# The opening of a streaming encoder step: the first two feature tiles as groups of their own, half-size loads and another order of the first steps

## The chip, the cores and the metric

The kernel runs on one core of a Trainium2 chip. The metric is the time of one execution on the device, in microseconds. A core has five engines that run their own instruction queues: TensorE (PE in the profile; its weight loads are PEld), VectorE (DVE), ScalarE (ACT), GpSimd (POOL) and SyncE (SP), which here issues the large loads. Engines wait for each other through semaphores; within an engine, instructions run in the order in which they were written.

## The reference

One layer of a hybrid encoder for two request groups, 256 frames of a new stream and 32 frames of a running one, all in fp32 with a width of 2048. What matters here is its beginning:

```python
def mixer_layer(x, c, conv_hist, ret_state, pos, ada_w, ada_b, g_pre, ...):
    mod = jax.nn.silu(c) @ ada_w + ada_b
    shift, scale, gate = jnp.split(mod, 3, axis=-1)
    h = rms_norm(x, g_pre) * (1.0 + scale[:, None]) + shift[:, None]
    proj = h @ w_in
    gb, gc, gu, zc, q, k, v, zr, ma, mb = jnp.split(proj, SPLIT_POINTS, axis=-1)
    ...
```

Behind it come a gated short convolution, a retention over eight heads, two branch products, an output product and a gated residual. The change touches none of these.

## The kernel before

**Tiles.** All 288 frames are kept with the features on the partitions: 16 feature tiles `kt` of 128 x 288. Products are made in fp32r, a rounded fp32, and each fp32 operand is split into a high and a low part, so that every product of a weight block and a tile of h is three matmuls: high by high (line 374), high by low (375) and low by high (378). Weights are split on the chip: ScalarE casts a piece of 128 x 1024 to `whi` (line 282), VectorE subtracts to get `wlo` (line 289). h is split in the same way into `hh` (line 346) and `hl` (line 352).

**The first stage.** Before the large loops the kernel makes h, and as each pair of feature tiles of h comes into being, multiplies it with the columns of q, k and of half of v (`FIRST`, three pieces of 1024 columns), and adds the results in SBUF in `firsts`. Eight groups `g` of two feature tiles (`GS = 2`) run one after the other. For each group the kernel needs 4 MB of `ada_w` (`ada_first`, four loads of 1 MB, each with four of the 16 feature tiles of c and the columns of shift and scale of this group) and 3 MB of `w_in` (`w_first`, three loads `u` of 1 MB, each two pieces). `modulate` (line 306) multiplies silu(c) with a load of `ada_first`, 8 instructions a load, and the last one copies the row to SBUF (`modrow`, line 310). `gather_mod` (line 316) turns it to the partitions, `factors` (lines 328 to 330) make a multiplier and an addend, `new_h` (lines 342 to 346) makes h and hh, `low_parts` hl.

**A block.** `multiply(i)` takes one load of `w_first`, that is, block (g, u). It goes in four steps j of two output tiles (a `pair` of PSUM banks, three of which turn). A step has 12 products; of each output tile they are: four with `whi` (both feature tiles with hh and hl), then `wlo` of the first feature tile, then `wlo` of the second. VectorE adds the pair into `firsts` (line 383; in group 0 it is copied, line 381). Then the step cuts further pieces ahead, as many as a small table says: `usual` is one after j = 1 and one after j = 3, and `rare` lists the blocks that differ. The blocks of a group run as (g, 0), (g, 1), the modulation of group g + 1, then (g, 2), in which h of the next group is made ahead of step 1; (g + 1, 0) follows at once.

**Order.** In this stage the order of all instructions on TensorE, ScalarE, VectorE and SyncE is the order of the Python program. Nine buffers `raw` hold the loads (the three tiles of x first), five each hold `whi` and `wlo`; load i + 8 is issued at the head of iteration i.

**The opening.** x is loaded in three pieces: `x[2]` (the 32 sample rows), `x[0]`, `x[1]`. ScalarE sums their squares (`square`, line 407), `norm` makes the mean (line 202, VectorE), the power -1/2 (line 204, GpSimd) and scales x (line 412, VectorE); `turn_x` transposes a piece on TensorE (line 422) and copies it to `xT` (line 424, VectorE or ScalarE). Lines 401 and 403 transpose the small vectors.

Of the kernel before, what the change touches and what calls it, by code (L numbers as in the profile page):

```python
# [36 lines left out]

GS, MOD = 2, 4
NG = NK // GS

# [52 lines left out]
def packed(c_prompt, c_sample, ada_b, state_conv, conv_w, conv_b, norm_pre, ada_w, w_in):  # L93


    rows = lambda *a: np.concatenate([np.reshape(v, (-1, P)) for v in a])
    small = rows(c_prompt, c_sample, ada_b[0, D:2 * D])
    table = rows(state_conv, conv_w, conv_b, norm_pre, ada_b[0, :D])
    a = ada_w[0, :, :2 * D].reshape(NK // MOD, MOD, P, 2, NG, GS * P)
    a = a.transpose(4, 0, 2, 1, 3, 5).reshape(NG, NK // MOD, P, MOD * 2 * GS * P)  # L100
    w = np.stack([w_in[0, :, c:c + PIECE] for c in FIRST]).reshape(len(FIRST), NG, GS, P, PIECE)
    w = w.transpose(1, 0, 3, 2, 4).reshape(NG, len(FIRST), P, GS * PIECE)
    return [np.ascontiguousarray(v) for v in (small, table, a, w)]


@with_exitstack
def hybrid_step(ctx: ExitStack, tc, x_prompt, x_sample, c_prompt, c_sample, state_conv, state_ret,
# [115 lines left out]
    with ExitStack() as phase:  # L223
# [25 lines left out]
        NU = len(FIRST)  # L249
        loads = [(True, 0, s) for s in range(NK // MOD)]  # L250
        for g in range(NG):
            m = [(True, g + 1, s) for s in range(NK // MOD)] if g + 1 < NG else []
            w = [(False, g, u) for u in range(NU)]
            loads += w[:2] + m + w[2:]
        raws, parts_of, mod_ps, state_of = {}, {}, {}, {}

        def load(i):
            if i >= len(loads):
                return
            is_mod, g, u = loads[i]  # L260
            raw = buffer("raw", KH * WC, F32, RAW, MORE_RAW)
            src = (ada_first if is_mod else w_first)[g, u]

            n = 2 if g == 0 and (is_mod or u == 0) else 1
            m = KH * WC // n
            for j in range(n):
                nc.sync.dma_start(out=raw[:, j * m:(j + 1) * m], in_=src[:, j * m:(j + 1) * m])
            if is_mod:
                raws[i] = raw.rearrange("p (k s c) -> p k s c", k=MOD, s=2)
            else:  # L270
                raws[i] = raw.rearrange("p (k c) -> p k c", k=GS)

        to_cut = [(i, k) for i, (is_mod, _, _) in enumerate(loads) if not is_mod for k in range(GS)]

# [9 lines left out]

        def cut_low():
            if half_cut:
                i, k, hi = half_cut.pop(0)
                lo = buffer("wlo", PIECE, F32R, PARTS, MORE_PARTS)
                V.tensor_tensor(out=lo, in0=raws[i][:, k], in1=hi.bitcast(F32), op=ALU.subtract)  # L289
                parts_of[i, k] = hi, lo  # L290

        def cut():
# [3 lines left out]
        def modulate(i):  # L296

            _, g, u = loads[i]
            if u == 0:
                mod_ps[g] = small_tile()  # L300
            pm, v = mod_ps[g], raws.pop(i)
            for k in range(MOD):
                kt = u * MOD + k
                for s in range(2):
                    at = 32 * (2 * (kt % 2) + s)
                    nc.tensor.matmul(pm[at:at + 32, :GS * P], cs[:, kt, :], v[:, k, s, :], start=kt < 2, stop=kt >= NK - 2,  # L306
                                     tile_position=(0, at))
            if u == NK // MOD - 1:
                ms = st.tile([P, GS * P], F32, name="modrow", tag="modrow", bufs=2)
                A.copy(out=ms, in_=pm[:, :GS * P])  # L310
                mod_ps[g] = ms

        def gather_mod(g):
            ms, po = mod_ps.pop(g), small_tile()
            for f in range(GS):
                nc.tensor.matmul(po[:, 4 * f:4 * f + 4], ms[:, f * P:(f + 1) * P], pick, start=True, stop=True)
            state_of[g] = po

        def factors(g):
            ks = slice(g * GS, (g + 1) * GS)  # L320
            mod = state_of[g][:, :4 * GS].rearrange("p (f s b) -> p f s b", s=2, b=2)
            mul = st.tile([P, GS, 2], F32, name="mul", tag="mul", bufs=2)
            add = st.tile([P, GS, 2], F32, name="add", tag="add", bufs=2)

            def each(v):
                return v.unsqueeze(2).broadcast_to([P, GS, 2])

# [5 lines left out]
        def new_h(g):  # L333
            mul, add = state_of[g]
            state_of[g] = hs = []
            for f in range(GS):
                h = st.tile([P, T], F32, name="h", tag="h", bufs=GS)
                kt = g * GS + f
                on_v = g == 0 and f == 1
                for b, c in enumerate((slice(0, TP), slice(TP, T))):  # L340
                    if on_v or (g == 0 and b):
# [4 lines left out]
                (V.tensor_copy if on_v else A.copy)(out=hh[:, kt, :], in_=h)  # L346
                hs.append(h)

        def low_parts(g):
            for f, h in enumerate(state_of.pop(g)):  # L350
                kt = g * GS + f
                V.tensor_tensor(out=hl[:, kt, :], in0=h, in1=hh[:, kt, :].bitcast(F32), op=ALU.subtract)  # L352


        usual, rare = {1: 1, 3: 1}, {(0, 0): {1: 1, 2: 1}, (0, 1): {3: 2}, (0, 2): {1: 1, 2: 1}, (1, 0): {1: 1, 2: 1, 3: 1}}

        def multiply(i):

            _, g, u = loads[i]
            parts = [parts_of.pop((i, k)) for k in range(GS)]  # L360
            cuts = rare.get((g, u), usual)
            nxt = u == NU - 1 and g + 1 < NG
            for j in range(NF // 2):
                if nxt and j == 1:
                    cut_high()
                    gather_mod(g + 1)
# [3 lines left out]
                for f in range(2):  # L370
                    ps, fs = pp[:, f, :T], slice((2 * j + f) * P, (2 * j + f + 1) * P)
                    for k, (hi, lo) in enumerate(parts):
                        kt = g * GS + k
                        nc.tensor.matmul(ps, hi[:, fs], hh[:, kt, :], start=k == 0, stop=False)  # L374
                        nc.tensor.matmul(ps, hi[:, fs], hl[:, kt, :], start=False, stop=False)  # L375
                    for k, (hi, lo) in enumerate(parts):
                        kt = g * GS + k
                        nc.tensor.matmul(ps, lo[:, fs], hh[:, kt, :], start=False, stop=k == GS - 1)  # L378
                sums = firsts[:, u * NF + 2 * j:u * NF + 2 * j + 2, :]
# [19 lines left out]
        xT = st.tile([P, NK, T], F32, name="xT")  # L399
        vp = small_tile()  # L400
        nc.tensor.transpose(out=vp[:, :3 * NK], in_=crows, identity=ident[:3 * NK, :3 * NK])
        vp2 = small_tile()
        nc.tensor.transpose(out=vp2[:, :NR * NK], in_=vrows, identity=ident)

# [8 lines left out]

        def turn_x(t):

            n = rows_of[t]
            m = 1024 // n if n < P else 8
            m = min(m, NK)
            for k0 in range(0, NK, m):
                pp = pair_tile().rearrange("p a b -> p (a b)")  # L420
                for k in range(m):
                    nc.tensor.transpose(out=pp[:, k * n:(k + 1) * n], in_=x[t][:n, (k0 + k) * P:(k0 + k + 1) * P],  # L422
                                        identity=ident[:n, :n])
                (V.tensor_copy if k0 or t == 2 else A.copy)(out=xT[:, k0:k0 + m, t * P:t * P + n],
                                                  in_=pp[:, :m * n].rearrange("p (k n) -> p k n", k=m))

        square(2)
        cv = vp[:, :2 * NK].rearrange("p (b k) -> p k b", b=2)
# [7 lines left out]
        ab1 = st.tile([P, NK], F32, name="ab1")  # L436
        V.tensor_scalar(out=ab1, in0=vp[:, 2 * NK:3 * NK], scalar1=1.0, scalar2=None, op0=ALU.add)
        V.tensor_copy(vecs, vp2[:, :NR * NK].rearrange("p (r k) -> p r k", r=NR))
        norm(0)
# [12 lines left out]
        new_h(0)  # L452
        cut_high()
        low_parts(0)
        cut_low()
        cut_low()

# [404 lines left out]
```

## Time and profile before

| | us |
|---|---|
| median of 3 runs (1353.58 to 1354.37) | 1353.85 |
| the profiled execution | 1354.2 |
| its span, from the first to the last instruction | 1352.4 |

The mean granted clock of TensorE over the span is 0.994. On the page, the busy time of an engine is also given as a share of the span, and the span is cut into 40 slices of 33.8 us, in which a digit is the busy share in tenths. The chain that ended last, by engine and by line:

```profile
PE 96%; DVE 2%; ACT 1%; DMA 1%; issue 0%; DVEq 0%; POOL 0%; POOLq 0%; ACTq 0%
PE acc L162 26%; PE acc L161 26%; PE acc L164 26%; PE pair L374 4%; PE pair L378 4%; PE pair L375 4%; PE small L306 2%; PE aux L665 1%; PE aux L508 0%; PE aux L509 0%; PE aux L510 0%; DVE wlo L289 0%; PE pair L422 0%; PE aux L610 0%; DMA state<-in_state_ret_dram 0%; PE aux L804 0%
```

The `acc` lines are the large loops behind the first stage, the `pair` lines the first stage. In the other views a row of a timeline gives the start, the time taken, the engine, the line, the operation, output <- inputs, shapes and a count; in brackets is the idle time of the engine ahead of it and what ended it. A row of windows gives for a stretch the busy time of PE, PEld, DVE, ACT and POOL, with the number of instructions, then the granted clock of TensorE, the busy share of the DMA engines and GB/s.

### The profile page before, as it was taken

What the parts mean: (1) busy time and instruction counts of PE and PEld (TensorE: products, weight loads), DVE (VectorE), ACT (ScalarE), POOL (GpSimd) and SP (SyncE); (2) the same over time, 40 slices, a digit from 0 to 9 for tenths busy, and PEclk for the clock granted to TensorE, in tenths of its full rate; (3) what the DMA queues carried; (4) which work ended last, traced back from release to release, by engine and by line L of the source; (5) the groups of instructions that cost most, each with busy time, mean ns of one, the idle gap of its engine ahead of it and who ended that gap; (6) DMA issues with size and microseconds to landing.
All of it is one profiled execution on the core that took longest, in us unless ns stands there. A gap on an engine that the chain in (4) does not pass through costs nothing.

```text
span 1352.4 us, 24163 instructions
## 1 busy us (share of the span) xinstructions
PE 1324.2 (98%) x10266; PEld 1302.0 (96%) x10266; DVE 834.1 (62%) x1380; ACT 547.5 (40%) x812; POOL 10.0 (1%) x18
## 2 busy tenths in 40 slices
PE   6999999999999999999999999999999999999996
PEld 5899899999999999999999999999999999999995
DVE  4667679865557766756877875555555544655443
ACT  4443346654444333333333333333333334334441
POOL 0000000000000000000000000000000000000000
PEclk8999999999999999999999999999999999999998
DMA  9988765455455675675666665544546355557431
GB/s 381 376 320 332 298 226 163 129 164 166 144 172 172 211 249 187 200 236 188 199 208 217 203 207 183 180 163 157 183 160 188 126 173 170 157 169 244 156 94 70
DMA packets 209116, 267.80 MB, mean 198 GB/s; under 512 B 5072, under 2 KB 199936, under 8 KB 201872
## 3 DMA queue, kind: packets, MB, share of 16 engines
q1 hardware_dynamic: 202784, 256.13, 55.9%
q10 hardware_dynamic: 6224, 10.13, 2.5%
q8 instruction: 80, 1.31, 0.4%
q14 instruction: 28, 0.23, 0.1%
HBM read 261.75 MB, written 4.49 MB: 197 GB/s over the span
## 4 chain that ended last, share of the span: by engine, by line
PE 96%; DVE 2%; ACT 1%; DMA 1%; issue 0%; DVEq 0%; POOL 0%; POOLq 0%; ACTq 0%
PE acc L162 26%; PE acc L161 26%; PE acc L164 26%; PE pair L374 4%; PE pair L378 4%; PE pair L375 4%; PE small L306 2%; PE aux L665 1%; PE aux L508 0%; PE aux L509 0%; PE aux L510 0%; DVE wlo L289 0%; PE pair L422 0%; PE aux L610 0%; DMA state<-in_state_ret_dram 0%; PE aux L804 0%
## 5 line engine op out<-in xcount | busy, mean ns | idle before, releaser
L127 DVE TENSOR_TENSOR wlo<-raw,whi 128x1024 fp32r<-128x1024 f32 x336 | 410.4, 1222 | 364.6 <-ACT whi L126 364.3
L126 ACT CAST whi<-raw 128x1024 fp32r<-128x1024 f32 x336 | 352.6, 1050 | 518.6 <-PE acc L162 471.3
L161 PE MATMUL acc<-hh,whi 128*128 128x288 f32 x1920 | 524.4, 296 | 0.9 <-DVE firsts L383 0.9
L162 PE MATMUL acc<-hl,whi 128*128 128x288 f32 x1920 | 525.0, 295 | 0.0
L161 PEld LDWEIGHTS acc<-hh,whi 128*128 128x128 f32 x1920 | 360.8, 188 | 1.4 <-ACT whi L126 1.1
L162 PEld LDWEIGHTS acc<-hl,whi 128*128 128x128 f32 x1920 | 361.1, 188 | 0.1
L164 PE MATMUL acc<-hh,wlo 128*128 128x288 f32 x1920 | 329.4, 293 | 0.0
L164 PEld LDWEIGHTS acc<-hh,wlo 128*128 128x128 f32 x1920 | 281.1, 188 | 0.0
L374 PE MATMUL pair<-hh,whi 128*128 128x288 f32 x384 | 110.3, 302 | 2.3 <-ACT hh L346 1.7
L375 PE MATMUL pair<-hl,whi 128*128 128x288 f32 x384 | 109.1, 299 | 0.1
L649 DVE SCALAR_TENSOR_TENSOR gbc<-raw,sc,gbc 128x256 f32<-128x256 f32 x240 | 100.5, 476 | 4.0 <-DMA raw<-in_ada_w_dram 3.9
L383 DVE TENSOR_TENSOR firsts<-pair,firsts 128x576 f32<-128x576 f32 x84 | 62.3, 753 | 39.4 <-PE pair L378 39.3
L378 PE MATMUL pair<-hh,wlo 128*128 128x288 f32 x384 | 84.1, 299 | 1.9 <-DVE wlo L289 1.8
L374 PEld LDWEIGHTS pair<-hh,whi 128*128 128x128 f32 x384 | 73.3, 191 | 5.8 <-issue 2.9
L375 PEld LDWEIGHTS pair<-hl,whi 128*128 128x128 f32 x384 | 73.4, 191 | 0.3 <-DVE hl L352 0.3
L162 PE MATMUL acc<-ml,whi 128*128 128x288 f32 x256 | 70.6, 297 | 0.0
L161 PE MATMUL acc<-mh,whi 128*128 128x288 f32 x256 | 70.1, 296 | 0.0
L161 PE MATMUL acc<-ch,whi 128*128 128x288 f32 x256 | 70.0, 296 | 0.0
L162 PE MATMUL acc<-yl,whi 128*128 128x288 f32 x256 | 70.0, 295 | 0.0
L161 PE MATMUL acc<-yh,whi 128*128 128x288 f32 x256 | 69.9, 296 | 0.0
L162 PE MATMUL acc<-cl,whi 128*128 128x288 f32 x256 | 69.5, 294 | 0.0
L378 PEld LDWEIGHTS pair<-hh,wlo 128*128 128x128 f32 x384 | 63.0, 191 | 3.1 <-DVE wlo L289 3.1
(182 smaller groups left out, 1316.3 us busy)
## 6 DMA issues: line engine op xcount, KB each, us to landing
raw<-in_w_in_dram SPq DMA_DIRECT2D x120, 1024.0 KB
raw<-in_w_branch_dram SPq DMA_DIRECT2D x32, 1024.0 KB
raw<-in_ada_first_dram SPq DMA_DIRECT2D x28, 1024.0 KB
raw<-in_w_first_dram SPq DMA_DIRECT2D x23, 1024.0 KB
raw<-in_ada_w_dram SPq DMA_DIRECT2D x16, 1024.0 KB
raw<-in_w_out_dram SPq DMA_DIRECT2D x16, 1024.0 KB
raw<-in_ada_first_dram SPq DMA_DIRECT2D x8, 512.0 KB
raw<-in_x_prompt_dram SPq DMA_DIRECT2D x2, 1024.0 KB
```

Of the source, the lines that this page charges most:

```text
L126: A.copy(out=hi, in_=src)
L127: V.tensor_tensor(out=lo, in0=src, in1=hi.bitcast(F32), op=ALU.subtract)
L161: nc.tensor.matmul(ps, hi[:, k, fs], xh[:, k0 + k, :], start=first and k == 0, stop=False)
L162: nc.tensor.matmul(ps, hi[:, k, fs], xl[:, k0 + k, :], start=False, stop=False)
L164: nc.tensor.matmul(ps, lo[:, k, fs], xh[:, k0 + k, :], start=False, stop=last and k == n - 1)
L306: nc.tensor.matmul(pm[at:at + 32, :GS * P], cs[:, kt, :], v[:, k, s, :], start=kt < 2, stop=kt >= NK - 2, tile_position=(0, at))
L374: nc.tensor.matmul(ps, hi[:, fs], hh[:, kt, :], start=k == 0, stop=False)
L375: nc.tensor.matmul(ps, hi[:, fs], hl[:, kt, :], start=False, stop=False)
L378: nc.tensor.matmul(ps, lo[:, fs], hh[:, kt, :], start=False, stop=k == GS - 1)
L383: V.tensor_tensor(out=sums, in0=pp[:, :, :T], in1=sums, op=ALU.add)
L649: V.scalar_tensor_tensor(out=ga[:, b], in0=raw[:, k], scalar=sc[:, kt, b:b + 1], in1=ga[:, b], op0=ALU.mult, op1=ALU.add)
L665: nc.tensor.matmul(pg[:, b, :], ones32, ga[:, b, :], start=True, stop=True)
```

## The change

The groups become `[[0], [1], [2, 3], [4, 5], ..., [14, 15]]`: tiles 0 and 1 are groups of their own, so there are nine groups, and what was group g of two tiles is now group g + 1. A one-tile group needs two loads of `ada_first` of 1 MB (eight feature tiles of c each, 128 columns of shift and of scale) and three loads of `w_first` of half a MB (one piece each); half-size loads take a whole buffer. A modulation step of such a group is half as wide and there are as many of them (32) as for two tiles. The arrays are packed on the host accordingly.

```diff
-GS, MOD = 2, 4
-NG = NK // GS
+GS = 2
+GROUPS = [[0], [1]] + [[k, k + 1] for k in range(2, NK, GS)]
+NG = len(GROUPS)
...
+        def shares(g):
+            return [(True, g, s) for s in range(2 * len(GROUPS[g]))] if g < NG else []
+
+        loads = shares(0)
         for g in range(NG):
-            m = [(True, g + 1, s) for s in range(NK // MOD)] if g + 1 < NG else []
+            m = shares(g + 1)
             w = [(False, g, u) for u in range(NU)]
             loads += w[:2] + m + w[2:]
...
-            n = 2 if g == 0 and (is_mod or u == 0) else 1
-            m = KH * WC // n
+            m = 2 if g == 0 and is_mod else 1
+            m = size // m
...
-        usual, rare = {1: 1, 3: 1}, {(0, 0): {1: 1, 2: 1}, (0, 1): {3: 2}, (0, 2): {1: 1, 2: 1}, (1, 0): {1: 1, 2: 1, 3: 1}}
+        usual = {1: 1, 3: 1}
+        rare = {(0, 0): {}, (0, 1): {0: 1, 2: 1, 3: 1}, (0, 2): {}, (1, 0): {}, (1, 1): {3: 3}, (1, 2): {}}
...
+                ahead = nxt and j == 1 and cuts.get(1)
                 if nxt and j == 1:
-                    cut_high()
+                    if ahead:
+                        cut_high()
                     gather_mod(g + 1)
...
                 if nxt and j == 1:
                     low_parts(g + 1)
-                    cut_low()
-                for _ in range(cuts.get(j, 0) - (nxt and j == 1)):
+                    if ahead:
+                        cut_low()
+                for _ in range(cuts.get(j, 0) - (1 if ahead else 0)):
                     cut()
...
+        def busy(ps, n):
+            for _ in range(n):
+                nc.tensor.transpose(out=ps, in_=ident, identity=ident)
...
+        busy(vp2[:, P:2 * P], 8)
         square(2)
...
-        V.tensor_copy(vecs, vp2[:, :NR * NK].rearrange("p (r k) -> p r k", r=NR))
+        turn_x(2, 1)
+        nc.tensor.transpose(out=vp2[:, :NR * NK], in_=vrows, identity=ident)
         norm(0)
-        turn_x(2)
+        V.tensor_copy(vecs, vp2[:, :NR * NK].rearrange("p (r k) -> p r k", r=NR))
+        turn_x(0, 2)
         norm(1)
-        turn_x(0)
         modulate(0)
-        turn_x(1)
+        turn_x(1, 2)
         for i in range(NBUF - len(x), NBUF - 1):
             load(i)
-        for i in range(1, NK // MOD):
-            modulate(i)
+        modulate(1)
+        idle = pair_tile()
+        busy(idle[:, 0, :P], 4)
         cut_high()
         gather_mod(0)
         factors(0)
+        busy(idle[:, 1, :P], 10)
         new_h(0)
-        cut_high()
+        low = low_steps(2)
+        next(low)
         low_parts(0)
-        cut_low()
-        cut_low()
+        next(low)
+        cut()
```

`low_steps(2)` subtracts the first `wlo` in two halves. In group 0 the sample columns of h are made on VectorE and all else of h and hh on ScalarE; before, VectorE also made the second tile. `busy` writes spare transposes of the identity, 22 in all, that nothing reads.

The opening on VectorE, from the constant ab1 to the copies of xT; `ms` and `raw` are the mean and the scaling of a piece of x, `vecs` the turned vectors. Before:

```order
L437 TENSOR_SCALAR ab1_146<-small_130 128x16
L438 COPY vecs_76<-small_132 128x128
L202 TENSOR_SCALAR ms_149<-ss_127 128x1
L412 TENSOR_SCALAR raw_102<-raw_102,rstd_151 128x2048
L424 COPY xT_129<-pair_154 128x16x32
L202 TENSOR_SCALAR ms_172<-ss_127 128x1
L412 TENSOR_SCALAR raw_103<-raw_103,rstd_174 128x2048
L424 COPY xT_129<-pair_187 128x8x128
L424 COPY xT_129<-pair_216 128x8x128
```

The same place in the changed kernel:

```order
L465 TENSOR_SCALAR ab1_150<-small_127 128x16
L451 COPY xT_126<-pair_152 128x16x32
L207 TENSOR_SCALAR ms_171<-ss_124 128x1
L440 TENSOR_SCALAR raw_102<-raw_102,rstd_173 128x2048
L469 COPY vecs_76<-small_128 128x128
L451 COPY xT_126<-pair_187 128x8x128
L207 TENSOR_SCALAR ms_197<-ss_124 128x1
L440 TENSOR_SCALAR raw_103<-raw_103,rstd_199 128x2048
L451 COPY xT_126<-pair_229 128x8x128
```

The copy of the transposed sample rows now stands ahead of the mean and the scaling of x[0], and the second copy of x[0] ahead of the mean and the scaling of x[1].

The seam from block (1, 0) to (1, 1) before, tiles 2 and 3, on VectorE; pair_601 is the last pair of (1, 0), pair_621 the first of (1, 1):

```order
L383 TENSOR_TENSOR firsts_85<-pair_583,firsts_85 128x576
L289 TENSOR_TENSOR wlo_599<-raw_290,whi_597 128x1024
L383 TENSOR_TENSOR firsts_85<-pair_601,firsts_85 128x576
L289 TENSOR_TENSOR wlo_617<-raw_453,whi_615 128x1024
L383 TENSOR_TENSOR firsts_85<-pair_621,firsts_85 128x576
```

The products of the first output tile of (1, 1) on TensorE before:

```order
L374 MATMUL pair_621<-hh_77,whi_579 128x288
L375 MATMUL pair_621<-hl_78,whi_579 128x288
L374 MATMUL pair_621<-hh_77,whi_597 128x288
L375 MATMUL pair_621<-hl_78,whi_597 128x288
L378 MATMUL pair_621<-hh_77,wlo_581 128x288
L378 MATMUL pair_621<-hh_77,wlo_599 128x288
```

The block reads wlo_581 and wlo_599; the split behind the sum of pair_601, the last of (1, 0), is wlo_617 of another load.

The same seam in the changed kernel, (2, 0) to (2, 1), also tiles 2 and 3, on VectorE; pair_689 is the last pair of (2, 0):

```order
L307 TENSOR_TENSOR wlo_673<-raw_466,whi_671 128x1024
L407 TENSOR_TENSOR firsts_85<-pair_675,firsts_85 128x576
L407 TENSOR_TENSOR firsts_85<-pair_689,firsts_85 128x576
L307 TENSOR_TENSOR wlo_705<-raw_466,whi_703 128x1024
L407 TENSOR_TENSOR firsts_85<-pair_709,firsts_85 128x576
```

And on TensorE, the products of the first output tile of (2, 1):

```order
L399 MATMUL pair_709<-hh_77,whi_671 128x288
L400 MATMUL pair_709<-hl_78,whi_671 128x288
L399 MATMUL pair_709<-hh_77,whi_703 128x288
L400 MATMUL pair_709<-hl_78,whi_703 128x288
L402 MATMUL pair_709<-hh_77,wlo_673 128x288
L402 MATMUL pair_709<-hh_77,wlo_705 128x288
```

The split that stands behind the sum of pair_689 is now one that this block reads.

More of the change, by code (lines that the diff above doesn't have):

```diff
@@ L98, in packed @@
     table = rows(state_conv, conv_w, conv_b, norm_pre, ada_b[0, :D])
[L99 to L103, printed above, removed]
+    shifts, firsts = [], []
+    for ks in GROUPS:
+        n, m = len(ks), KH * GS // (2 * len(ks))
+        c = slice(ks[0] * P, (ks[-1] + 1) * P)
+        a = ada_w[0, :, :2 * D].reshape(NK // m, m, P, 2, D)[..., c]
+        shifts.append(a.transpose(0, 2, 1, 3, 4).ravel())
+        w = np.stack([w_in[0, c, f:f + PIECE] for f in FIRST]).reshape(len(FIRST), n, P, PIECE)
+        firsts.append(w.transpose(0, 2, 1, 3).ravel())
+    return [np.ascontiguousarray(v) for v in (small, table, np.concatenate(shifts), np.concatenate(firsts))]
 @with_exitstack
@@ L260, in load @@
             is_mod, g, u = loads[i]
-            raw = buffer("raw", KH * WC, F32, RAW, MORE_RAW)
-            src = (ada_first if is_mod else w_first)[g, u]
-            n = 2 if g == 0 and (is_mod or u == 0) else 1
-            m = KH * WC // n
-            for j in range(n):
-                nc.sync.dma_start(out=raw[:, j * m:(j + 1) * m], in_=src[:, j * m:(j + 1) * m])
+            n = len(GROUPS[g])
+            size = KH * WC if is_mod else n * PIECE
+            raw = buffer("raw", KH * WC, F32, RAW, MORE_RAW)[:, :size]
             if is_mod:
-                raws[i] = raw.rearrange("p (k s c) -> p k s c", k=MOD, s=2)
+                at = GROUPS[g][0] * 2 * P * D + u * P * size
             else:
-                raws[i] = raw.rearrange("p (k c) -> p k c", k=GS)
-        to_cut = [(i, k) for i, (is_mod, _, _) in enumerate(loads) if not is_mod for k in range(GS)]
+                at = GROUPS[g][0] * P * PIECE * NU + u * P * size
+            src = (ada_first if is_mod else w_first)[at:at + P * size].rearrange("(p c) -> p c", p=P)
+            m = 2 if g == 0 and is_mod else 1
+            m = size // m
+            for j in range(0, size, m):
+                nc.sync.dma_start(out=raw[:, j:j + m], in_=src[:, j:j + m])
+            if is_mod:
+                raws[i] = raw.rearrange("p (k s c) -> p k s c", s=2, c=n * P)
+            else:
+                raws[i] = raw.rearrange("p (k c) -> p k c", k=n)
+        to_cut = [(i, k) for i, (is_mod, g, _) in enumerate(loads) if not is_mod for k in range(len(GROUPS[g]))]
         half_cut = []
@@ L283, in cut_high, with low_steps @@
                 half_cut.append((i, k, hi))
-        def cut_low():
+        def low_steps(halves):
             if half_cut:
@@ L288, in cut_low @@
                 lo = buffer("wlo", PIECE, F32R, PARTS, MORE_PARTS)
-                V.tensor_tensor(out=lo, in0=raws[i][:, k], in1=hi.bitcast(F32), op=ALU.subtract)
                 parts_of[i, k] = hi, lo
+                m = PIECE // halves
+                for c in range(0, PIECE, m):
+                    V.tensor_tensor(out=lo[:, c:c + m], in0=raws[i][:, k, c:c + m], in1=hi[:, c:c + m].bitcast(F32), op=ALU.subtract)
+                    if halves > 1:
+                        yield
+        def cut_low():
+            for _ in low_steps(1):
+                pass
         def cut():
@@ L301, in modulate @@
             pm, v = mod_ps[g], raws.pop(i)
-            for k in range(MOD):
-                kt = u * MOD + k
+            n, m = len(GROUPS[g]), v.shape[1]
+            for k in range(m):
+                kt = u * m + k
                 for s in range(2):
                     at = 32 * (2 * (kt % 2) + s)
-                    nc.tensor.matmul(pm[at:at + 32, :GS * P], cs[:, kt, :], v[:, k, s, :], start=kt < 2, stop=kt >= NK - 2,
+                    nc.tensor.matmul(pm[at:at + 32, :n * P], cs[:, kt, :], v[:, k, s, :], start=kt < 2, stop=kt >= NK - 2,
                                      tile_position=(0, at))
-            if u == NK // MOD - 1:
+            if kt == NK - 1:
                 ms = st.tile([P, GS * P], F32, name="modrow", tag="modrow", bufs=2)
-                A.copy(out=ms, in_=pm[:, :GS * P])
+                A.copy(out=ms[:, :n * P], in_=pm[:, :n * P])
                 mod_ps[g] = ms
@@ L314, in gather_mod @@
             ms, po = mod_ps.pop(g), small_tile()
-            for f in range(GS):
+            for f in range(len(GROUPS[g])):
                 nc.tensor.matmul(po[:, 4 * f:4 * f + 4], ms[:, f * P:(f + 1) * P], pick, start=True, stop=True)
@@ L319, in factors @@
         def factors(g):
[L320 to L323, printed above, removed]
+            n = len(GROUPS[g])
+            ks = slice(GROUPS[g][0], GROUPS[g][0] + n)
+            mod = state_of[g][:, :4 * n].rearrange("p (f s b) -> p f s b", s=2, b=2)
+            mul = st.tile([P, GS, 2], F32, name="mul", tag="mul", bufs=2)[:, :n]
+            add = st.tile([P, GS, 2], F32, name="add", tag="add", bufs=2)[:, :n]
             def each(v):
-                return v.unsqueeze(2).broadcast_to([P, GS, 2])
+                return v.unsqueeze(2).broadcast_to([P, n, 2])
             V.tensor_tensor(out=mul, in0=mod[:, :, 1, :], in1=each(ab1[:, ks]), op=ALU.add)
@@ L335, in new_h @@
             state_of[g] = hs = []
-            for f in range(GS):
+            for f, kt in enumerate(GROUPS[g]):
                 h = st.tile([P, T], F32, name="h", tag="h", bufs=GS)
-                kt = g * GS + f
-                on_v = g == 0 and f == 1
                 for b, c in enumerate((slice(0, TP), slice(TP, T))):
-                    if on_v or (g == 0 and b):
+                    if g == 0 and b:
                         V.tensor_scalar(out=h[:, c], in0=xT[:, kt, c], scalar1=mul[:, f, b:b + 1],
@@ L345, in new_h @@
                         A.activation(h[:, c], xT[:, kt, c], AF.Identity, scale=mul[:, f, b:b + 1], bias=add[:, f, b:b + 1])
[L346 removed]
+                A.copy(out=hh[:, kt, :], in_=h)
                 hs.append(h)
         def low_parts(g):
[L350 to L351 removed]
+            for kt, h in zip(GROUPS[g], state_of.pop(g)):
                 V.tensor_tensor(out=hl[:, kt, :], in0=h, in1=hh[:, kt, :].bitcast(F32), op=ALU.subtract)
[L355 removed]
+        usual = {1: 1, 3: 1}
+        rare = {(0, 0): {}, (0, 1): {0: 1, 2: 1, 3: 1}, (0, 2): {}, (1, 0): {}, (1, 1): {3: 3}, (1, 2): {}}
         def multiply(i):
             _, g, u = loads[i]
[L360 removed]
+            ks = GROUPS[g]
+            parts = [parts_of.pop((i, k)) for k in range(len(ks))]
             cuts = rare.get((g, u), usual)
```

24 lines of the change are left out of this document (9 added, 15 removed).

## The prediction

> **What bounds the kernel now.** I read the page first: the busy line, then the slices.
>
> ```profile
> span 1352.4 us, 24163 instructions
> PE 1324.2 (98%) x10266; PEld 1302.0 (96%) x10266; DVE 834.1 (62%) x1380; ACT 547.5 (40%) x812; POOL 10.0 (1%) x18
> ...
> PE   6999999999999999999999999999999999999996
> ```
>
> TensorE is busy for 98% of the span; only the first and the last slice fall under 9. The change touches the first stage alone, so the second view is the windows, cut where that stage ends. The end of the stage comes from the view of line 378: its last product starts at 213.0 us.
>
> ```profile
> 0.00:213.40 213.40, 199.98 (x1746) 182.11 (x1746) 140.26 (x212) 86.81 (x123) 2.38 (x9) 0.98 0.79 311
> 213.40:1352.40 1139.00, 1124.19 (x8520) 1119.88 (x8520) 693.89 (x1169) 460.67 (x690) 7.66 (x9) 1.00 0.55 177
> ...
> L378 PE MATMUL pair<-hh,wlo x384: 288/295/608, 25.5 to 213.0; 128*128 128x288 f32 x192
> ```
>
> TensorE idles 213.40 - 199.98 = 13.4 us in this stage, almost all of it before the first product. Whatever moves the end of this stage moves the end of the kernel, since behind it TensorE is busy for 98.7%. So two questions decide: when does the stage start its products, and does TensorE wait between them.
>
> **The opening.** The third view is the timeline of the first 24 us.
>
> ```profile
> 8.51 1.92 PE L422 MATMUL pair<-ident,raw 32*128 32x32 f32 x16
> 9.01 0.15 DVE L202 TENSOR_SCALAR ms<-ss 128x1 f32<-128x1 f32 x1
> 9.85 1.28 DVE L412 TENSOR_SCALAR raw<-raw,rstd 128x2048 f32<-128x2048 f32 x1 [0.68 <-POOL rstd L204]
> ...
> 11.05 0.68 DVE L424 COPY xT<-pair 128x512 f32<-128x512 f32 x1
> ...
> 11.19 3.67 PE L422 MATMUL pair<-ident,raw 128*128 128x128 f32 x16 [0.76 <-DVE raw L412]
> ...
> 14.79 1.32 PE L306 MATMUL small<-raw,cs 128*32 128x256 f32 x16
> 16.04 1.97 PE L422 MATMUL pair<-ident,raw 128*128 128x128 f32 x16
> 17.93 2.80 PE L306 MATMUL small<-raw,cs 128*32 128x256 f32 x48
> 18.04 1.23 DVE L424 COPY xT<-pair 128x1024 f32<-128x1024 f32 x1 [1.92 <-PE pair L422]
> ...
> 23.51 0.40 PE L374 MATMUL pair<-hh,whi 128*128 128x288 f32 x1 [1.68 <-ACT hh L346]
> ```
>
> Before, VectorE norms x[0] at 9.85 and copies the transposes of the sample rows afterwards. Now the copy stands ahead of the norm (order rows of the opening). It waits for TensorE until 8.51 + 1.92 = 10.43 and takes 0.68, so it ends at 11.1. From the mean (line 202) to the norm are 9.85 - 9.01 = 0.84 by way of GpSimd, the norm takes 1.28: done at 13.3 where it was 11.13, **2.1 us later**. The transposes of x[0] then run 13.3 to 17.0 (3.67). The next norm stands behind the second copy of these (1.23, to 18.2); with 0.84 and 1.28 it is done at 20.3, and the transposes of x[1] (1.97) end at 22.3, where they ended at 18.0. What is saved stands behind that: modulation of one tile is 32 instructions of half width, of which 16 are left, where the last 24 took 2.80 (two records each). Half of them at full price are 1.87, at half price 0.93. So the last ends at about 23.7 instead of 20.73. From there to the first product were 23.51 - 20.73 = 2.78; I keep that, since the copy of the row, the gather, the factors, h and hh remain in a row. First product: **26.5 instead of 23.51**, with 25 (clock full from the first transposes) and 29.5 (clock half throughout) as ends.
>
> The spare transposes cost nothing there: 8 lie before 8.51, where TensorE has nothing; 4 and 10 take 0.12 each at the price of the third transposes row (1.97 for 16), 1.7 in all, inside the 2.78; at the price of the row before (3.67 for 16) they would stick out by about half a us. The transposes at 11.19 took 0.23 each, those at 16.04 0.12: the clock doubled after a stretch of transposes with only one modulation step in it. [...]
>
> Next, from the first product to tile 2, which both kernels take as the first of a pair.
>
> ```profile
> 42.39 3.66 PE L306 MATMUL small<-raw,cs 128*32 128x256 f32 x64
> ...
> 52.41 2.36 DVE L289 TENSOR_TENSOR wlo<-raw,whi 128x1024 fp32r<-128x1024 f32 x2
> ...
> 53.54 0.40 PE L374 MATMUL pair<-hh,whi 128*128 128x288 f32 x1 [0.15 <-ACT whi L282]
> ...
> 53.92 0.29 PE L378 MATMUL pair<-hh,wlo 128*128 128x288 f32 x1
> 54.82 0.40 PE L378 MATMUL pair<-hh,wlo 128*128 128x288 f32 x1 [0.61 <-DVE wlo L289]
> 55.05 0.29 PE L374 MATMUL pair<-hh,whi 128*128 128x288 f32 x1
> ```
>
> Before: 53.54 - 23.51 = 30.0 us, of which 144 products at 0.132 (pitch below) are 19.0 and one modulation 3.6; the other 7.4 are waits for split pieces and products at half clock. Now: 19.0, the modulation of tiles 2 and 3 (3.6), that of tile 1 in half-width steps (1.8 to 3.6; I take 2.7), two gathers (0.6) and some 2 us of waits: 27.9. Tile 2 starts at 54.4, **0.9 later** (from -2 to +4 with the ends above). Loads don't bind: by tile 2 the same bytes are needed at the same time, and half-size loads come in the order of use. Tile 1 adds 12 sums on VectorE (9 us at 0.75), each beside 6 products of 0.79, so they are covered.
>
> **The split pieces.** This is the main term. A piece of weights (128x1024) is split into whi on ScalarE and wlo on VectorE; `multiply` of a pair of tiles needs two. Before, the special rows of `rare` put three cuts into (1, 0), so VectorE was one piece ahead for the rest of the stage: in the order rows of before, wlo_617, the last ahead of group 1's second block, isn't used there; pair_621 uses wlo_581 and wlo_599. Counting the new table: two pieces ahead of the loop, three in (0, 1), three in (1, 1), two per block from (2, 0) on; (2, 1) needs pieces 8 and 9, and the second is cut in the last quarter of (2, 0). The order rows show it: wlo_705 is the sixth operand of the first products of pair_709, and on VectorE it stands **behind the sum of pair_689**, the last products before. So at each seam TensorE must drain, VectorE sum, then split, and only then TensorE goes on. The cost at a seam is read from places where VectorE did these two steps in this order:
>
> ```profile
> 107.11 0.43 PE L378 MATMUL pair<-hh,wlo 128*128 128x288 f32 x2
> 107.38 0.29 PE L374 MATMUL pair<-hh,whi 128*128 128x288 f32 x1
> ...
> 107.92 0.43 PE L378 MATMUL pair<-hh,wlo 128*128 128x288 f32 x2
> ...
> 107.57 0.76 DVE L383 TENSOR_TENSOR firsts<-pair,firsts 128x576 f32<-128x576 f32 x1 [0.56 <-PE pair L378]
> 108.25 1.22 DVE L289 TENSOR_TENSOR wlo<-raw,whi 128x1024 fp32r<-128x1024 f32 x1
> ```
>
> After the last products (107.11) the sum starts at 107.57, the split ends at 108.25 + 1.22 = 109.47, and TensorE starts 0.05 later (54.77 to 54.82 above): 109.52. The sixth product of the next block would start at 107.92 + 0.13 = 108.05. Wait: 1.47, and 0.10 for the start out of a wait (54.82 to 55.05 is 0.23 instead of 0.13): **1.57**. It stands at (2, 1) to (8, 1), seven times, and at (8, 2), where no modulation lies between: eight, 12.6 us. Between (g, 1) and (g, 2) 3.6 us of modulation hide it.
>
> At (3, 0) to (8, 0) VectorE is also behind, because h of the next group came just before:
>
> ```profile
> 101.01 0.29 PE L374 MATMUL pair<-hh,whi 128*128 128x288 f32 x1
> 101.53 0.43 PE L378 MATMUL pair<-hh,wlo 128*128 128x288 f32 x2
> ...
> 101.34 1.41 DVE L383 TENSOR_TENSOR firsts<-pair,firsts 128x576 f32<-128x576 f32 x2
> 102.67 1.21 DVE L289 TENSOR_TENSOR wlo<-raw,whi 128x1024 fp32r<-128x1024 f32 x1
> ```
>
> The block starts at 101.01 (six products in 0.79, to the next at 101.80: 0.132 each), its sixth product at 101.66; the split behind the last sum ends at 103.88. Before, this piece wasn't needed yet; now it is: 103.93 - 101.66 = 2.27, with 0.10 **2.37**, six times: 14.2 us. ScalarE's half isn't late, since its cuts wait for no sum. The bounds of these 14 waits are nothing (if the pieces were ready) and these figures plus 0.3 each; rows and order leave no reason for less, so I take 26.8.
>
> **The clock.** Such waits can halve the clock, as one did here:
>
> ```profile
> 25.00:26.00 1.00, 0.93 (x3) 0.45 (x3) 1.00 (x2) 0.00 (x0) 0.00 (x0) 0.80 1.04 434
> 32.00:33.00 1.00, 1.00 (x8) 1.00 (x7) 1.00 (x2) 0.00 (x0) 0.00 (x0) 0.79 0.98 410
> ...
> 18.77:22.18 3.41, 2.57 (x43) 1.43 (x32) 0.77 (x4) 1.38 (x2) 0.00 (x0) 1.00 1.05 417
> 22.18:25.59 3.41, 1.41 (x5) 0.75 (x5) 3.34 (x10) 2.09 (x4) 0.00 (x0) 1.00 1.00 416
> 25.59:29.01 3.42, 2.85 (x11) 2.52 (x12) 1.00 (x1) 0.28 (x1) 0.00 (x0) 0.50 1.01 422
> 29.01:32.42 3.41, 3.41 (x16) 3.41 (x16) 0.81 (x2) 1.30 (x2) 0.00 (x0) 0.50 1.01 420
> ```
>
> The granted clock fell at 25.6 and rose at 32.4, twice 3.41 us later. The stretch of 3.41 before the fall was busy for 41%; one that was busy for 75% brought no fall; one at 83% brought no rise, a full one did. A wait of 2.27 shows as about 2.1 idle (the last product's record outlasts its pitch by 0.16); whole inside a stretch it leaves 38% busy, which falls. That happens to (3.41 - 2.1)/3.41 = 38% of six; with those split between stretches I take three falls, each one stretch at half clock, a loss of 1.7: 5.1 us. A short wait leaves at least 62%, between the two known shares: unknown, a rival.
>
> **Sum:** 0.9 + 12.6 + 14.2 + 5.1 = 32.8 on the profiled execution's own 1354.2 us (span 1352.4 and 1.8 around it; the median of the runs is 1353.85): **1387.0**.
>
> **Rivals.** (b) The clock never falls at these waits: 27.7, 1381.9. The fall at 25.6 came with no wait longer than the 1.68 before the first product, which speaks against it. [...] (c) Short waits make it fall too: 62% of eight and four of six, nine falls at 1.7 to 2.6, some 19 us: 1401. (d) The opening runs at half clock, the spare transposes don't do what they are for: first product at 29.5, 3 more: 1390. (e) Faster: tile 0 needs only half the modulation, and its loads land 5 us earlier (2.1 MB less at the 416 GB/s of the second stretch). If the norms were not late and the clock stayed full in the opening, about 5 us would be gained: 1349, provided the 14 waits don't come. It decides below 5/14 = 0.35 us a seam; the wait at 54.82 was 0.61 in a far milder place.
>
> **How the numbers follow.** Forecast 47%, (b) 18%, (c) 20%, (d) 8%, (e) 5%, no change 2%. The range 1379 to 1402 leaves out (e), no change, a little of (b) and half of (c). Measurements tell 0.2% (2.7 us) from no change: faster 5%, same 2%, slower 93%.
>
> **What would show it.** Right: the first product at 26 to 27 us, tile 2 at 54 to 55; then waits of TensorE for wlo, two in each group of two tiles, 1.3 and 2.1 us as recorded; the stage's last product at 240 to 247 instead of 213; the same 98.7% behind it. Wrong: wlo done before its sixth product (no waits), or more than six stretches at half clock.

## The result, and the profile after

| | us |
|---|---|
| before, median of 4 runs (1353.58 to 1354.53) | 1354.11 |
| after, median of 4 runs (1384.69 to 1387.63) | 1386.76 |
| the profiled execution after; its span | 1386.69; 1384.9 |

The change makes the kernel slower: the ratio after to before is 1.0239, with an interval of 1.0227 to 1.0251. The page of the changed kernel, its busy line, its slices and the group of its late products (in a group: busy time and mean ns, then the idle time ahead and what ended it):

```profile
span 1384.9 us, 24356 instructions
...
PE 1333.2 (96%) x10352; PEld 1308.9 (95%) x10352; DVE 844.6 (61%) x1393; ACT 548.5 (40%) x816; POOL 10.0 (1%) x18
...
PE   6998888999999999999999999999999999999996
...
L402 PE MATMUL pair<-hh,wlo 128*128 128x288 f32 x384 | 91.0, 303 | 22.9 <-DVE wlo L307 22.9
```

The span grew by 32.5 us. TensorE has four slices with an 8, the fourth to the seventh (104 to 242 us, at 34.6 us a slice), where before it had only nines, and 22.9 us of its idle time stand ahead of line 402, ended by VectorE's split. The view of that line tells how often and until when (duration least/median/most, first and last start), and the waits of TensorE put it at the head of their list, with the number and the longest:

```profile
L402 PE MATMUL pair<-hh,wlo x384: 288/295/607, 27.8 to 244.0; 128*128 128x288 f32 x192
```

```profile
PE pair L402 <- DVE wlo L307: 22.9, 14, 2.1
```

Fourteen waits; the stage's last product stands at 244.0 instead of 213.0, so 31.0 of the 32.5 us arise in this stage. One seam of each kind in the timeline; first (2, 0) to (2, 1), then (2, 2) to (3, 0):

```profile
61.65 0.43 PE L402 MATMUL pair<-hh,wlo 128*128 128x288 f32 x2
...
62.12 0.76 DVE L407 TENSOR_TENSOR firsts<-pair,firsts 128x576 f32<-128x576 f32 x1 [0.60 <-PE pair L402]
...
62.45 0.29 PE L402 MATMUL pair<-hh,wlo 128*128 128x288 f32 x1
62.79 1.21 DVE L307 TENSOR_TENSOR wlo<-raw,whi 128x1024 fp32r<-128x1024 f32 x1
...
64.06 0.40 PE L402 MATMUL pair<-hh,wlo 128*128 128x288 f32 x1 [1.32 <-DVE wlo L307]
...
80.76 1.42 DVE L407 TENSOR_TENSOR firsts<-pair,firsts 128x576 f32<-128x576 f32 x2
...
80.95 0.35 PE L402 MATMUL pair<-hh,wlo 128*128 128x288 f32 x1
82.09 1.22 DVE L307 TENSOR_TENSOR wlo<-raw,whi 128x1024 fp32r<-128x1024 f32 x1
...
83.36 0.40 PE L402 MATMUL pair<-hh,wlo 128*128 128x288 f32 x1 [2.06 <-DVE wlo L307]
```

The order reads off the starts: the last products of a block (61.65), the sum (62.12), the split (62.79, done at 64.00), and 0.06 later the sixth product of the next block. At the long seam VectorE has two sums to do first.

The windows show what the waits do to the clock. The columns are those of the windows before; each stretch is 3.41 us long and placed in step with the falls of the granted clock, which this execution has at 19.79, 84.64 and 139.25: 19 and 16 times 3.41 us apart.

```profile
81.23:84.64 3.41, 1.34 (x10) 1.28 (x10) 2.12 (x4) 1.86 (x2) 0.00 (x0) 1.00 1.02 432
84.64:88.05 3.41, 3.41 (x17) 3.41 (x16) 1.47 (x3) 0.00 (x0) 0.00 (x0) 0.50 0.81 310
108.53:111.95 3.42, 1.58 (x12) 1.34 (x10) 3.42 (x4) 3.28 (x4) 0.00 (x0) 1.00 1.02 429
135.84:139.25 3.41, 1.49 (x11) 1.26 (x10) 3.41 (x4) 3.20 (x4) 0.00 (x0) 1.00 1.01 428
139.25:142.67 3.42, 3.28 (x13) 3.28 (x14) 0.85 (x2) 0.00 (x0) 0.00 (x0) 0.50 0.88 314
...
60.75:64.16 3.41, 2.09 (x17) 1.85 (x15) 2.66 (x4) 1.05 (x1) 0.00 (x0) 1.00 1.02 425
```

Behind the stretches at 81.23 and 135.84, busy for 39% and 44%, the clock is halved for one stretch (0.50 at 84.64 and 139.25). Behind 108.53 (46%) it is not, nor behind a stretch with a short wait, at 60.75 (61%).

The opening, from the timeline of TensorE:

```profile
13.32 3.43 PE L449 MATMUL pair<-ident,raw 128*128 128x128 f32 x16 [2.40 <-DVE raw L440]
16.69 1.08 PE L330 MATMUL small<-raw,cs 128*32 128x128 f32 x32
20.24 3.37 PE L449 MATMUL pair<-ident,raw 128*128 128x128 f32 x16 [2.48 <-DVE raw L440]
23.55 1.08 PE L330 MATMUL small<-raw,cs 128*32 128x128 f32 x32
...
27.07 0.40 PE L399 MATMUL pair<-hh,whi 128*128 128x288 f32 x1 [0.53 <-ACT hh L369]
...
54.21 0.31 PE L399 MATMUL pair<-hh,whi 128*128 128x288 f32 x1
```

TensorE waits 2.40 and 2.48 us for the two norms, the first product is at 27.07 instead of 23.51, and tile 2 starts at 54.21.

### The profile page after: what moved, and what is told of

It is laid out like the page before. It is cut to its first block, busy times and chain, and to the rows that moved or that the text cites. A ratio compares the mean times of both kernels' runs of the same rounds, so it can differ in the third digit from the quotient of the medians.

```text
span 1384.9 us, 24356 instructions
## 1 busy us (share of the span) xinstructions
PE 1333.2 (96%) x10352; PEld 1308.9 (95%) x10352; DVE 844.6 (61%) x1393; ACT 548.5 (40%) x816; POOL 10.0 (1%) x18
## 3 DMA queue, kind: packets, MB, share of 16 engines
q8 instruction: 81, 1.33, 0.5%
## 4 chain that ended last, share of the span: by engine, by line
PE 90%; DVE 6%; ACT 2%; DMA 1%; issue 1%; POOL 0%; DVEq 0%; POOLq 0%; ACTq 0%
PE acc L167 25%; PE acc L166 25%; PE acc L169 25%; PE pair L402 3%; PE pair L400 3%; PE pair L399 3%; PE small L330 2%; DVE wlo L307 2%; DVE firsts L407 1%; ACT h L368 1%; PE pair L449 1%; DMA state<-in_state_ret_dram 1%; ACT hh L369 1%; PE aux L697 0%; DVE wlo L132 0%
## 5 line engine op out<-in xcount | busy, mean ns | idle before, releaser
L407 DVE TENSOR_TENSOR firsts<-pair,firsts 128x576 f32<-128x576 f32 x96 | 72.0, 756 | 68.2 <-PE pair L402 67.5
L402 PE MATMUL pair<-hh,wlo 128*128 128x288 f32 x384 | 91.0, 303 | 22.9 <-DVE wlo L307 22.9
```

The source lines that it names most:

```text
L407: V.tensor_tensor(out=sums, in0=pp[:, :, :T], in1=sums, op=ALU.add)
```

## The experiments

Two theories stood against each other. **The seams:** the new table has VectorE no piece ahead, and the waits for its splits are nearly all of the loss; the halved clock is a small addition. **The grouping:** one-tile groups with narrow steps, or the new opening, cost the time themselves, and the waits only show it. The first three kernels tell these apart. Ratios are to the kernel before, run on the same chip beside each.

**One piece ahead again.** The changed kernel with one cut more in (2, 0):

```diff
-        rare = {(0, 0): {}, ..., (1, 1): {3: 3}, (1, 2): {}}
+        rare = {(0, 0): {}, ..., (1, 1): {3: 3}, (1, 2): {}, (2, 0): {1: 1, 2: 1, 3: 1}}
```

> The changed kernel with one entry more in its table: block (2, 0) cuts three pieces instead of two, so VectorE is a piece ahead again from there on. If the 14 waits at the seams and the clock falls that they bring are the loss, they go (26.5 us of waits with their restarts, 3.4 us of falls in the profiled run), the stage's last product comes at 213 to 215 and the time is 1355 to 1357. If the loss were in the one-tile groups or the half-size loads themselves (12 more sums on VectorE, buffers half filled), the time would stay above 1375.

Measured: 1355.82 (1354.51 to 1356.28, 11 runs), ratio 1.0011 (1.0002 to 1.0020). The first product is at 27.44, tile 2 at 54.60, much as in the changed kernel, yet the waits are gone. The groups of this kernel's page, and its view of line 402:

```profile
L402 PE MATMUL pair<-hh,wlo 128*128 128x288 f32 x384 | 85.9, 294 | 0.0
```

```profile
L402 PE MATMUL pair<-hh,wlo x384: 288/295/399, 28.2 to 214.7; 128*128 128x288 f32 x192
```

One entry of the table takes the end of the stage from 244.0 to 214.7. The longest product of this line takes 399 ns instead of 607.

**The kernel before without its lead.** The reverse, with groups of two tiles and the old opening:

```diff
-... {(0, 0): {1: 1, 2: 1}, (0, 1): {3: 2}, (0, 2): {1: 1, 2: 1}, (1, 0): {1: 1, 2: 1, 3: 1}}
+... {(0, 0): {1: 1, 2: 1}, (0, 1): {3: 2}, (0, 2): {1: 1, 2: 1}}
```

> The kernel before, with the one special entry of block (1, 0) taken out, so it cuts two pieces there as everywhere. Nothing else of the change is in it. Seams: if the lead of one piece alone is the matter, 14 waits appear ((1, 1) to (7, 1), (2, 0) to (7, 0), (7, 2)), 1.3 and 2.1 us as recorded, and the time is 1380 to 1386. If the loss needs the one-tile groups, it stays within 3 us of 1354.

Measured: 1384.30 (1383.06 to 1385.36, 4 runs), ratio 1.0222 (1.0208 to 1.0236). From its timeline, one short and one long wait, and the windows around the second:

```profile
62.01 0.40 PE L378 MATMUL pair<-hh,wlo 128*128 128x288 f32 x1 [1.33 <-DVE wlo L289]
...
81.33 0.59 PE L378 MATMUL pair<-hh,wlo 128*128 128x288 f32 x1 [2.07 <-DVE wlo L289]
```

```profile
77.97:81.38 3.41, 1.34 (x11) 1.11 (x9) 3.31 (x4) 3.01 (x4) 0.00 (x0) 1.00 1.01 425
81.38:84.80 3.42, 3.42 (x14) 3.42 (x15) 0.76 (x1) 0.00 (x0) 0.00 (x0) 0.50 0.93 359
```

So the same waits, 1.33 and 2.07, come without any one-tile group, at the same kind of seam. The long one leaves its stretch busy for 39%, and the next runs at half clock. The grouping falls as a cause of the waits; the lost lead alone makes 2.2%.

**The lead, and the norms first.** The first experiment, with both norms ahead of the copies and transposes that the change had put before them:

```diff
+        norm(0)
         turn_x(2, 1)
         nc.tensor.transpose(out=vp2[:, :NR * NK], in_=vrows, identity=ident)
-        norm(0)
+        norm(1)
         V.tensor_copy(vecs, vp2[:, :NR * NK].rearrange("p (r k) -> p r k", r=NR))
         turn_x(0, 2)
-        norm(1)
         modulate(0)
```

> As the kernel with one piece ahead, and the means and scalings of x[0] and x[1] again ahead of the copies of the transposes on VectorE. If the order of the opening costs what the working of the prediction says (2.1 us at the first norm, 6.5 at the second), the first product comes 4 to 5 us earlier, at 22 to 23, and the time is 1350 to 1352. If the loads set the start instead, the first product stays later than 25 and the time stays above 1354.

Measured: 1349.92 (1349.44 to 1350.86, 6 runs), ratio 0.9970 (0.9959 to 0.9982), 5.9 us under the first experiment, a little under the expected 1350, and the lowest median here. Its timeline of the opening:

```profile
11.12 3.68 PE L449 MATMUL pair<-ident,raw 128*128 128x128 f32 x16 [0.32 <-DVE raw L440]
...
16.59 2.11 PE L449 MATMUL pair<-ident,raw 128*128 128x128 f32 x16
...
22.16 0.40 PE L399 MATMUL pair<-hh,whi 128*128 128x288 f32 x1 [0.53 <-ACT hh L369]
```

The waits for raw of 2.40 and 2.48 have become 0.32 and nothing; the first product is at 22.16 and tile 2 at 49.30.

**The waits filled.** The changed kernel with spare transposes in the fourteen waits; they take nothing away and wait for nothing:

```diff
+    if kt == ks[-1] and j == f == 0 and g > 1 and (u == 1 or u == 0 and g > 2 or g == NG - 1 and u):
+        for _ in range(12 if u else 19):
+            nc.tensor.transpose(out=pp[:, 1, :P], in_=ident, identity=ident)
     nc.tensor.matmul(ps, lo[:, fs], hh[:, kt, :], start=False, stop=kt == ks[-1])
```

> The changed kernel with spare transposes in the 14 waits (12 in the short ones, 19 in the long ones, 0.11 us each, written where the pair's second half is overwritten later), so TensorE is busy in them. The waits stay. If they halve the clock now and then and transposes count as busy, the clock does not fall between 30 us and the end of the stage, and the time is that of the changed kernel less 1.7 us for each fall: 1382.5 to 1384. If transposes do not count for the clock, falls stay as in the changed kernel and the time is 1385 to 1388.

Measured: 1382.88 (1381.89 to 1383.74, 4 runs), ratio 1.0211 (1.0198 to 1.0225), just clear of the changed kernel's. The timeline at the seam, where the products are still held back as long as before, and the windows of the whole stage:

```profile
61.31 0.30 PE L405 MATMUL pair<-hh,wlo 128*128 128x288 f32 x1
61.44 1.47 PE L404 MATMUL pair<-ident 128*128 128x128 f32 x12
62.93 0.40 PE L405 MATMUL pair<-hh,wlo 128*128 128x288 f32 x1
```

```profile
18.90:240.20 221.30, 217.89 (x1971) 199.63 (x1968) 143.83 (x207) 79.47 (x118) 0.17 (x1) 1.00 0.71 270
```

The clock never fell in these 221 us, and the end of the stage went from 244.0 to 239.9: 1.1 of these 4.1 us stand ahead of the first product (25.94), where the clock of the changed kernel had fallen at 19.8, and 2.9 at the waits. By this estimate its two falls at the waits cost about 1.45 each, apart from the waits themselves.

It doesn't show that the spare transposes held the clock there. By the author's placing of the stretches, each long wait of this execution lies across two. The one that would be the least busy without them runs from 80.43; it is busy for all of its 3.41 us, and this row of it counts line 404 alone, the spare transposes (busy time of PE and PEld, then as before):

```profile
80.43:83.84 3.41, 1.83 (x17) 1.59 (x15) 1.00 1.02 430
```

Without them about 1.6 us would be left, as much as in the stretch at 108.53 of the changed kernel (1.58), behind which the clock held too.

**Without the spare transposes.** The fastest kernel with none of the change's spare transposes (`range(n)` becomes `range(0)`):

> As the kernel with one piece ahead and the norms first, with none of the 22 spare transposes: what is left of the change is the one-tile groups, the half-size loads and the new table. If the spare transposes only hold the clock, the first product comes at 22 as with them, the clock falls once or is released later within the first 40 us in most runs, and the time is 1350.5 to 1353. If they do nothing (transposes not counted), it is 1349.5 to 1350.3, as with them.

Measured: 1350.95 (1349.63 to 1351.42, 7 runs), ratio 0.9971 (0.9960 to 0.9983). The clock falls behind the stretch that the transposes had filled (with them, in the third experiment, TensorE was busy for 14.78 of the 15.40 us from 14.60 on, and the clock stayed at 1.00):

```profile
20.17:23.58 3.41, 1.64 (x11) 1.34 (x11) 2.89 (x8) 2.76 (x5) 0.00 (x0) 1.00 1.01 407
23.58:26.99 3.41, 3.41 (x16) 3.41 (x15) 1.35 (x2) 1.15 (x2) 0.00 (x0) 0.50 1.05 426
```

The stage ends at 210.7 instead of 209.4, but the ratio can't be told from that with them (0.9970). So the rows show the clock lower without them in these two executions, 0.50 against 1.00; a gain in time is not shown here.

**The kernel before with late norms.** Its opening with each norm behind the copies, as the change has it:

```diff
-        norm(0)
         turn_x(2)
-        norm(1)
+        norm(0)
         turn_x(0)
+        norm(1)
```

> The kernel before with the order of the opening alone changed on VectorE: the scaling of x[0] behind the copy of the sample rows, that of x[1] behind the copy of x[0]. By the working of the prediction the second scaling ends 6.5 us later; 6 of the modulation's 8 steps stand behind the transposes that follow, so the first product moves from 23.5 to 27 to 29 and the time is 1357 to 1360. If the loads of the first group set its start anyway (4 MB land by 20 us), the first product moves by less than 1.5 us and the time stays below 1355.5.

Measured: 1360.21 (1358.30 to 1360.31, 5 runs), ratio 1.0039 (1.0026 to 1.0051), that is 5.8 us over the 1354.37 beside it, and the first product at 29.62, both a little past what was expected. With the 5.9 of the third experiment this gives the price of the late norms from both sides.

**The kernel before with spare transposes.** Four ahead of the gather, fourteen behind the factors:

```diff
+        idle = pair_tile()
...
+        busy(idle[:, 0, :P], 4)
         cut_high()
...
         factors(0)
+        busy(idle[:, 1, :P], 14)
         new_h(0)
```

> The kernel before with 18 spare transposes ahead of its first product (4 before the gather, 14 behind it) and nothing else. Its clock fell at 25.6 us and rose at 32.4 in the profiled run, about 3 us of loss. If the transposes hold the clock, the fall goes or is shorter in some runs: 1351 to 1353.3. If not, 1353.5 to 1354.5.

Measured: 1352.20 (1351.21 to 1355.46, 11 runs), ratio 0.9990 (0.9982 to 0.9999). Its windows, beside those of the kernel before:

```profile
14.02:30.00 15.98, 14.38 (x139) 10.76 (x139) 8.01 (x15) 6.29 (x9) 0.00 (x0) 1.00 1.03 419
```

```profile
14.02:30.00 15.98, 12.56 (x107) 8.92 (x107) 7.07 (x13) 5.93 (x9) 0.00 (x0) 0.86 1.02 416
```

In this stretch the clock stays at 1.00 where it was 0.86 without them. One stretch of 3.41 us of it, first with all engines, then with line 453 alone, the spare transposes:

```profile
20.85:24.26 3.41, 2.95 (x21) 2.29 (x20) 2.70 (x10) 2.77 (x4) 0.00 (x0) 1.00 1.03 419
```

```profile
20.85:24.26 3.41, 1.78 (x15) 1.60 (x14) 1.00 1.03 419
```

Outside the spare transposes 2.95 - 1.78 = 1.17 us of this stretch are busy; the records of all else add up to 1.4, with what overlaps them. In the kernel before, the clock fell behind a stretch busy for 1.41, and in the changed kernel behind one of 1.49; here it held. But this execution is the fastest of the eleven. Six have a mean clock of 0.996 and take 1351.21 to 1352.20 us; five have 0.994 or 0.995 and take 1353.78 to 1355.46, as the kernel before does at 0.993 or 0.994. By these clocks the transposes helped in six of the eleven executions, and the gain in the median is 0.1%, at the edge of what can be told.

**Ahead at the end only.** The stage's end was well told by then, but the part behind it took 1.5 us more than before. The only waits there that the kernel before doesn't have are 0.2 more for y and one of 0.7 on line 642 in the changed kernel, which VectorE's line 636 ends. Theory: VectorE leaves the first stage late, having no lead, and brings this with it. So the changed kernel with a lead in the last group alone:

```diff
-... (1, 2): {}}
+... (1, 2): {}, (8, 0): {1: 1, 2: 1, 3: 1}}
```

> The changed kernel with the third cut in block (8, 0) only, so VectorE gets its piece ahead just before the stage ends. The waits at (8, 1) and (8, 2) go, 12 stay: 3.2 us less in the stage. From the last product of the stage to the end of the span, the kernels with a piece ahead took 1138.7 to 1139.8 us, those without 1140.4 to 1142.1. If VectorE's lateness at the end of the stage makes that difference, this kernel takes 1138.7 to 1139.8 behind the stage, and its time is 1381 to 1383.5; if something earlier does, it takes 1140.4 or more and its time is 1383 to 1385.

Measured: 1379.51 (1377.65 to 1382.50, 4 runs), ratio 1.0191 (1.0174 to 1.0208). Twelve waits for wlo remain, that of line 642 is gone, and from the last product of the stage to the end of the span it is 1139.4 us (1140.9 in the changed kernel, 1139.5 before). The theory holds. The time came out lower than expected, for another reason: in the profiled execution the clock fell at none of the long waits (it is 1.00 from 24.20 to 238.50). The windows around the one that begins at 81.5:

```profile
78.78:82.19 3.41, 2.71 (x21) 2.48 (x19) 2.75 (x5) 3.38 (x6) 0.00 (x0) 1.00 1.00 418
82.19:85.60 3.41, 2.05 (x15) 2.05 (x16) 2.07 (x3) 1.01 (x2) 0.00 (x0) 1.00 0.96 389
```

The wait ends with the same 2.06 as in the changed kernel, but lies across two stretches, which stay busy for 79% and 60%. In the changed kernel the wait that begins at 81.30 lies whole in the stretch from 81.23; here the one from 81.5 on crosses the end of a stretch at 82.19.

## Why the prediction was right

The direction, the mechanism and the total held: 1387.0 predicted, 1386.69 in the profiled execution, 1386.76 in the median. By its steps, on the profiled executions:

| term | predicted, us | measured, us |
|---|---|---|
| start of tile 2 | +0.9 | +1.25 |
| 14 waits at the seams | 26.8 | 26.9 |
| falls of the clock | 5.1 | 2.9 |
| behind the stage | 0 | +1.5 |
| sum | 32.8 | 32.5 (the spans differ by 32.5) |

- **The seams.** The recorded waits are eight of about 1.32 and six of about 2.06, 22.9 together. A short one costs 0.16 more than recorded (a product is recorded with 0.29 at a pitch of 0.13), a long one 0.22 (the product ahead of it is recorded with 0.35, as the row at 80.95 is), and each 0.10 for the start out of the wait: 22.9 + 8 x 0.26 + 6 x 0.32 = 26.9. The first two experiments show that the lost lead is the cause, from both sides.
- **The opening: mis-sized twice.** The start of tile 2 before was read wrongly: the prediction took 53.54, where the row shows a product ended by a wait; that is the third product of its block, and the first stands at 52.96:

```profile
52.69 0.43 PE L378 MATMUL pair<-hh,wlo 128*128 128x288 f32 x2
52.96 0.30 PE L374 MATMUL pair<-hh,whi 128*128 128x288 f32 x1
53.10 0.29 PE L375 MATMUL pair<-hl,whi 128*128 128x288 f32 x1
```

  The new block's start was right (54.4 predicted, 54.21 measured), so the term is 54.21 - 52.96 = 1.25. The first product came at 27.07 instead of 26.5: the clock fell at 19.8, in the wait for the second norm, and was 0.50 to 23.2, so the transposes of x[1] took 3.37 where 1.97 was assumed. The narrow modulation steps came back cheaper than the middle taken: 32 records in 1.08. The late norms were worked out as 3.0 at the first product, net of the cheaper steps; undone, they are worth 5.9 in the time (third and sixth experiments). And of the 13.4 us that TensorE idles in the stage of the kernel before, 10.7 stand ahead of the first product (it is busy for 12.85 of these 23.51 us) and 2.8 behind it, so "almost all" was too much.
- **The falls.** Two at the waits instead of three, and 2.9 for both (fourth experiment, with the same waits) instead of 1.7 each. This term was mis-sized, and it is one of chance: long waits of 2.06 brought two falls in the changed kernel's execution and none in the last experiment's, where the stretches begin elsewhere. That the total came within 0.3 us is luck in part, since this term was 2.2 too large while the start of tile 2 and the part behind the stage were 1.9 too small.
- **Behind the stage.** Not predicted: that 98.7% of that part is TensorE's work was read as no change there. But VectorE's lateness at the end of the stage is carried over it, and costs 1.5 (last experiment). Nearly all of it arises at line 642. Here are the products around these six transposes, first before, then in the changed kernel:

```profile
280.98 0.69 PE L164 MATMUL acc<-hh,wlo 128*128 128x288 f32 x4
...
282.08 0.38 PE L161 MATMUL acc<-hh,whi 128*128 128x288 f32 x1
```

```profile
311.98 0.69 PE L169 MATMUL acc<-hh,wlo 128*128 128x288 f32 x4
313.35 1.33 PE L642 MATMUL aux<-ident,on 128*128 128x128 f32 x6 [0.68 <-DVE on L636]
314.44 0.38 PE L166 MATMUL acc<-hh,whi 128*128 128x288 f32 x1
```

  Ahead of the transposes the changed kernel is 31.0 us later, just what the stage costs; behind them it is 32.4 later. So the 0.2 more for y doesn't show there, and the recorded wait of 0.68 is only half of what this place costs.

**The rivals.** That the clock never falls at these waits (b) is refuted by the two stretches at half clock, though the last experiment's profiled execution went that way (1.00 from 24.20 to 238.50). That short waits make it fall too (c) is refuted by the stretch at 60.75, with 61% busy and the clock held at 1.00, and by the two falls at the waits instead of nine. The opening at half clock (d) was part right: one stretch of it was (0.50 from 19.79 to 23.20), with 1.4 us lost in the transposes of x[1]. The faster case (e) needed the seams to vanish and the norms not to be late; the third experiment made both so, and measured 1349.92 against its 1349.

The spare transposes: the prediction read a doubled clock from two rows of transposes, 0.23 and 0.12 us each. In the changed kernel the sixteen at 20.24, at a granted clock of 0.50, took 3.37, that is 0.21 each, which agrees; the windows of the kernel before print 1.00 for both of its rows, so there the times alone show it. In the opening the clock held behind a stretch in which all but the spare transposes takes 1.4 us (seventh experiment, 1.00 from 14.02 to 30.00), and without any it fell to 0.50 behind the stretch that they had filled (fifth, at 23.58). For the waits it stays open. The fourth experiment's 221.30 us at 1.00 can't decide it, since the last experiment's profiled execution had no fall at the long waits either, with nothing in them.

## What to carry to other kernels

When a table of cuts written by hand is regrouped, count at every seam how many pieces the producer is ahead of the reader: with none, each seam costs the drain, the sum and the split in a row, here 1.6 to 2.4 us fourteen times, and one entry of the table mends it. Test a regrouping apart from the edits of order that come with it: here the grouping with its lead and with early norms makes the kernel 0.3% faster, the late norms cost 5.9 us, and the lost lead 31 with its falls of the clock. And read the first product of a block by its place in the block's pattern, not by the row with the wait.

## What the hardware showed beside that

- In the changed kernel the clock fell behind stretches of 3.41 us that TensorE was busy for 1.34 and 1.49 us (at 81.23 and 135.84), and held behind one of 1.58 (at 108.53). But it fell behind one of 1.58 in the sixth experiment (at 27.51) and behind 1.64 in the kernel without spare transposes (at 20.17). So the recorded busy time gives no sharp edge here. In the profiled executions of the kernel before and of the changed kernel, from 15.35 and 16.37 us on, the clock fell behind each stretch at full clock that was busy for 44% or less, and held behind each of 46% (108.53), 55% (166.56) and more. A wait of 2.06 us was enough where it lay whole inside a stretch (at 81.23).
- A modulation step of half width cost little more than half here: 32 records take 1.08 us, where 48 of full width (two for a step) took 2.80, that is 0.034 and 0.058 each.
- The runs of the changed kernel spread in step with their mean clock: 1384.69 us at a mean clock of 0.995, 1386.69 and 1386.83 at 0.993, 1387.63 at 0.992.
